# Rotary scores as 128-row products, rotary queries ahead of the heads, and a written order on four engines where attention hands over to decode and w_o

## The chip, the cores and the metric

The kernel runs on one core of one Trainium2 chip. The metric is device time in microseconds of one execution. Engines are named as in the profile: PE (TensorE) multiplies matrices, DVE (VectorE) and ACT (ScalarE) work on tiles, POOL (GpSimd) and SP (SyncE) mostly issue DMAs here; each engine works through its own queue in order. PEclk is the clock that TensorE was granted, as a share of full speed.

## The reference, cut

One step of a two-layer decoder. Layer 0 is latent attention (MLA) over 1024 new prompt tokens and, for 8 sequences with 4 new tokens each, over a paged cache of 8192 rows. Layer 1 is a gated DeltaNet, and each layer is followed by a SwiGLU FFN. Norms stand ahead of and behind every sublayer. What the change touches is layer 0:

```python
a = u @ w_in                                   # 1024 -> 384 + 256 + 64
c_q  = rmsnorm(a[..., :384], g_q)
c_kv = rmsnorm(a[..., 384:640], g_kv)
k_r  = rope(a[..., 640:], pos)                 # one rotary key of 64, shared by 8 heads
q = (c_q @ w_uq).reshape(b, t, 8, 128 + 64)    # per head: 128 plain + 64 rotary
q_rope = rope(q[..., 128:], pos)
s = (q_lat . c_kv + q_rope . k_r) * SCALE      # causal softmax over keys
...
o = (p @ c_kv) @ w_uv ;  mix = o @ w_o
h = x + rmsnorm(mix, nw1);  u = rmsnorm(h, nw2);  FFN(u)
```

## The kernel before

All products are in fp32 precision: each operand is split into a high part (ACT rounds it, `wh`, `qh`) and a low part (DVE subtracts, `wl`, `ql`), and three products hi·hi, lo·hi, hi·lo stand for one (L258, L259, L260 in `mm3`, called by `lin`). The split is `split` (L233 on ACT, L234 on DVE). Tokens are columns: groups GRP of 384, 384 and 288 (1024 prompt and 32 decode tokens). On PE the instructions stand in written order inside `order()`; the other engines' order, and that of PE outside, is set by the scheduler from the program.

**Projections** (`mla_latents`, until about 184 us). Behind the latents come four pairs of heads. For each pair: the pair's rotary queries (`mla_w_uqr`, three groups, ACT copies them to `qr`), then its two heads' plain queries (`mla_w_uqn`, each split into `qh`, `ql` and stored to DRAM `qd`). The rotation needs the swapped halves of `qr`: `swap` loads them by four DMAs (L602, issued on ACT's queue) into `araw`, and `rotate` makes three DVE passes (L607 to L609). `qrs` keeps the decode columns; high and low part go to DRAM `qrd`. The key's rotation (`raw[5]`) stands behind pair 1 and gives KRh (high part, in both halves of the rows) and KR (64 rows of high part, 64 of low part). Eight PSUM banks hold the projections.

**Prompt attention** (184 to 438 us, `mla_attend`). For each pair, `att_pair` loads its queries from DRAM on SP; `att_scores` scores 128 queries of one head against up to 512 keys a chunk: three plain products, one rotary product of the high query part on KR (128 rows: the query's high part stacked twice, so that both key parts count), the causal mask where the chunk holds the diagonal, and one rotary product of the low query part on KRh with 64 rows:

```python
mm(o, x["q1"][e][:, qsl], KR[:, c], start=False, stop=False)      # L1026
mm(o, x["q2"][r, qsl], KRh[r, c], start=False, stop=True)         # L1029, r: 64 rows
```

Then DVE takes the maximum, ACT the exponential, DVE normalises, PE transposes and multiplies with the values. Head outputs go to DRAM `oT`.

**Handover** (438 to 465 us). The heads come back from DRAM as `uo` (`oh`, `ol`), and `Decode` attends over the cache pages in 66 steps: `scores` (PE products L1746 to L1755, DVE maximum, ACT exponential `dpr`), `turn` (PE transposes L1790, ACT copies to `dpt`), `values` (PE, L1807). Two steps run first; then `wo_half` multiplies the first 768 columns by w_o, one column block `m` at a time, and `ffn_half` follows. In these, `aside` puts decode steps between the groups of products: each call does `turn`, adds RATE to a credit and does `scores` when it reaches one. POOL's order is written here, that of ACT, DVE and SP is the scheduler's.

**Norms** (`boundary_group`). Behind w_o come the sum of squares of the post-norm (on PE, L409), the residual (`hld` loads `xT` on SP, NHL buffers), squares `sqr` and, GAP groups later, the sum of the second norm, then `u`.

Of the kernel before, what the change touches and what calls it, by code (L numbers as in the profile page):

```python
# [15 lines left out]
P = 128  # L16
# [21 lines left out]
NHL = 5, 3  # L38
GAP = 1, 3
# [10 lines left out]
FW = (2, 3), (3, 4), (2, 4)  # L50
# [7 lines left out]
RATE = 0.55  # L58
# [45 lines left out]
class K:  # L104


    def __init__(self, ctx, tc, I, O):
# [8 lines left out]
        self.side, self.credit = None, 0.0  # L116
# [31 lines left out]
    def aside(self, middle=False):  # L148

        if self.side is None:  # L150
            return
        if middle:
            self.side.values()
            return
        self.side.turn()
        self.credit += RATE
        if self.credit >= 1 and self.side.scores():
            self.credit -= 1
# [103 lines left out]
    def lin(self, out, w, x, col, g, m=P):  # L262
# [7 lines left out]
        self.aside()  # L270

# [365 lines left out]
    def first_layer(self, right, top, h1, h2):  # L637
# [4 lines left out]
        with ExitStack() as left:  # L642
# [19 lines left out]
            for h, d in [(7, 1), (5, 0), (5, 1)] + [(h, d) for h in (0, 1, 2, 3, 4, 6, 7) for d in range(2)]:  # L662
                uo[h][d].half(0)
            acc, hid = ([Two(lambda: self.half(self.aa, 0, F32, "acc", 8), lambda i=i: self.half(self.ab[i], 1, F32, "acc", 8))
                         for _ in range(KD)] for i in range(2))
            with self.banks(**DBANK):
                with self.order(mybir.EngineType.Pool):


                    self.side = Decode(self, *smp, OL, tab, msk, wk)  # L670
                    pages = self.side.load

                    def heads(eng, *hd):
                        for h, d in hd:
                            eng.dma_start(uo[h][d].half(0).bitcast(F32), oT[h][d][:, :TA])

                    heads(nc.sync, (6, 0), (6, 1), (7, 0))
                    pages(1, 1, 0, 2, False)
# [3 lines left out]
                    pages(0, 1, 0, 4)  # L682
                    pages(1, 1, 2, 3)
                    heads(nc.gpsimd, (0, 0), (0, 1), (1, 0), (1, 1), (2, 0), (2, 1), (3, 0), (3, 1), (4, 0))
                    pages(0, 0, 0, 3)
                    pages(1, 1, 3, 4)
                    pages(0, 0, 3, 4)
                    heads(nc.sync, (7, 1))
                    heads(nc.gpsimd, (4, 1), (5, 0), (5, 1))
                    pages(1, 0, 0, 4)  # L690
                    for _ in range(2):
                        self.side.scores()
                        self.side.turn()
                        self.side.values()
                with self.order():
                    u, r2, start = self.boundary(acc, I["xT"], h1, (0, 1), (0, 2), uo, full)
                    self.kstep = KSTEP[1]
                    self.wo_half(uo, acc, gA, start, first)
# [8 lines left out]
                    for _ in range(9):  # L707
# [6 lines left out]
        with self.scope("ab") as self.ab[0], self.weights(*FW[1], side="left"), self.order(), self.banks(ps=8), \  # L714
                self.scope("ffn", "right") as self.fp:
            self.queue, self.gap = nc.gpsimd, GAP[1]
            for h, x in enumerate(uo):
                for d in range(2):
                    nc.sync.dma_start(x[d].half(1)[:, :TP - TA].bitcast(F32), oT[h][d][:, TA:])
# [14 lines left out]
    def wo_half(self, uo, acc, gs, start, first=()):  # L734
# [3 lines left out]
        first = list(first)  # L738
        for g in gs:
            for m in range(KD):  # L740
                ps = self.psum()
                self.lin(ps, self.weight(self.I["mla_w_o"][m], raw=first.pop(0) if first else None), uo, 0, g)
# [47 lines left out]
    def mla_latents(self, u, r2, start, ws, araw, gn, wk, cst):  # L790
        nc, I, O, tc, NH = self.nc, self.I, self.O, self.tc, 8
        with self.banks(ps=8):
# [32 lines left out]

            ckv = [(self.S(F32R, "kvh"), self.S(F32R, "kvl")) for _ in range(2)]
            KRh, KR = self.S(F32R, "KRh"), self.S(F32R, "KR")
# [8 lines left out]
            for p in range(NH // 2):  # L836
                qr, sw = self.S(F32, "qr"), araw(p % 2)
                for h in (None, 2 * p, 2 * p + 1):
                    w = self.weight(I["mla_w_uqr"][p] if h is None else I["mla_w_uqn"][h], 384)
                    if h is not None:  # L840
                        hl = self.S(F32R, "qh"), self.S(F32R, "ql")
                    for g in GRP:
                        self.ready(("q", g[0]))
                        ps = self.psum()
                        self.lin(ps, w, cq, 0, g)
                        n = min(g[1], TP - g[0])
                        s = slice(g[0], g[0] + n)
                        if h is None:
# [1097 lines left out]
```

## Time and profile before

| | |
|---|---|
| median of 3 runs | 3182.97 us (3180.69 to 3184.98) |
| profiled execution | 3181.79 us, its span 3180.1 us |
| granted clock, mean over the span | 0.978 |
| PE busy | 3062.9 us, 96% |
| DVE, ACT, POOL busy | 1835.7, 1170.1, 493.8 us |
| DMA | 432.42 MB, mean 136 GB/s |

In rows of the timeline the first number is the start in us, the second the duration (which overlaps the next for pipelined matmuls), then engine, line, operation, out<-in, shapes, and in brackets the idle time ahead of it with what ended it. A row of a window has its length, then busy us and instructions of PE, PE's weight loads, DVE, ACT and POOL, then PEclk, the DMA engines' share and GB/s.

### The profile page before, as it was taken

What the parts mean: (1) busy time and instruction counts of PE and PEld (TensorE: products, weight loads), DVE (VectorE), ACT (ScalarE), POOL (GpSimd) and SP (SyncE); (2) the same over time, 40 slices, a digit from 0 to 9 for tenths busy, and PEclk for the clock granted to TensorE, in tenths of its full rate; (3) what the DMA queues carried; (4) which work ended last, traced back from release to release, by engine and by line L of the source; (5) the groups of instructions that cost most, each with busy time, mean ns of one, the idle gap of its engine ahead of it and who ended that gap; (6) DMA issues with size and microseconds to landing.
All of it is one profiled execution on the core that took longest, in us unless ns stands there. A gap on an engine that the chain in (4) does not pass through costs nothing.

```text
span 3180.1 us, 57805 instructions
## 1 busy us (share of the span) xinstructions
PE 3062.9 (96%) x21526; PEld 2807.7 (88%) x21526; DVE 1835.7 (58%) x4234; ACT 1170.1 (37%) x2545; POOL 493.8 (16%) x897
## 2 busy tenths in 40 slices
PE   8999979999999999999999999999989999999998
PEld 8878857788888889999898888888789999999997
DVE  7667745634444444786676666666476444444436
ACT  5344434553333323454344444443443111111122
POOL 1200123343334321121011111111000000000000
PEclk9989989999999999999999999999999999999999
DMA  3553369988788854365422222223341111111113
GB/s 123 195 186 98 110 198 308 294 276 268 243 263 273 265 184 144 105 226 174 129 63 81 71 73 63 65 76 104 96 139 60 54 40 54 40 54 40 40 54 110
DMA packets 284987, 432.42 MB, mean 136 GB/s; under 512 B 60513, under 2 KB 220129, under 8 KB 284706
## 3 DMA queue, kind: packets, MB, share of 16 engines
q1 hardware_dynamic: 219138, 272.41, 26.7%
q0 software_dynamic: 45232, 141.92, 13.8%
q10 hardware_dynamic: 20336, 14.39, 1.5%
q8 instruction: 170, 2.79, 0.4%
q14 instruction: 111, 0.91, 0.1%
HBM read 367.59 MB, written 58.30 MB: 134 GB/s over the span
## 4 chain that ended last, share of the span: by engine, by line
PE 83%; DVE 8%; DMA 4%; issue 2%; ACT 2%; SPq 1%; POOL 0%; DVEq 0%; ACTq 0%; POOLq 0%
PE ps L258 21%; PE ps L260 21%; PE ps L259 21%; PE po L1807 2%; PE sc L1751 2%; PE tp L1056 1%; DMA w<-ffn_w_in 1%; PE sc L1029 1%; DVE wl L234 1%; PE sc L1755 1%; PE sc L1023 1%; PE s L1626 1%; ACT ga L1410 1%; PE s L1623 1%; DMA w<-mla_w_o 1%
## 5 line engine op out<-in xcount | busy, mean ns | idle before, releaser
L258 PE MATMUL ps<-oh,wh 128*128 128x384 f32 (+1 forms) x2496 | 823.2, 330 | 2.5 <-ACT wh L233 1.5
L260 PE MATMUL ps<-oh,wl 128*128 128x384 f32 (+1 forms) x2496 | 810.5, 325 | 2.0 <-DVE wl L234 2.0
L259 PE MATMUL ps<-ol,wh 128*128 128x384 f32 (+1 forms) x2496 | 808.7, 324 | 0.0
L233 ACT ACTIVATE wh<-w 128x1024 fp32r<-128x1024 f32 (+3 forms) x302 | 300.2, 1002 | 647.9 <-PE ps L259 497.0
L258 PEld LDWEIGHTS ps<-oh,wh 128*128 128x128 f32 x2496 | 473.6, 190 | 31.6 <-issue 28.0
L260 PEld LDWEIGHTS ps<-oh,wl 128*128 128x128 f32 x2496 | 472.9, 189 | 2.8 <-DVE wl L234 2.7
L259 PEld LDWEIGHTS ps<-ol,wh 128*128 128x128 f32 x2496 | 473.1, 190 | 1.3 <-issue 0.8
L234 DVE TENSOR_TENSOR wl<-w,wh 128x1024 fp32r<-128x1024 f32 (+3 forms) x299 | 343.0, 1155 | 149.9 <-ACT wh L233 145.7
L1723 POOL DMA_DIRECT2D pg<-cache x524 | 286.8, 547 | 438.7 <-PE po L1807 345.4
L258 PE MATMUL ps<-uh,wh 128*128 128x384 f32 (+1 forms) x912 | 312.1, 343 | 7.6 <-ACT wh L233 7.6
L259 PE MATMUL ps<-ul,wh 128*128 128x384 f32 (+1 forms) x912 | 307.9, 338 | 1.6 <-DVE ul L340 1.6
L260 PE MATMUL ps<-uh,wl 128*128 128x384 f32 (+1 forms) x912 | 303.0, 332 | 1.5 <-POOL wl L234 1.5
L258 PE MATMUL ps<-hh,wh 128*128 128x384 f32 (+1 forms) x880 | 294.1, 336 | 0.2 <-ACT hh L233 0.2
L259 PE MATMUL ps<-hl,wh 128*128 128x384 f32 (+1 forms) x880 | 289.9, 330 | 0.2 <-DVE hl L234 0.2
L260 PE MATMUL ps<-hh,wl 128*128 128x384 f32 (+1 forms) x880 | 289.3, 329 | 0.0
L258 PEld LDWEIGHTS ps<-uh,wh 128*128 128x128 f32 x912 | 175.0, 192 | 11.4 <-ACT wh L233 7.6
L259 PEld LDWEIGHTS ps<-ul,wh 128*128 128x128 f32 x912 | 175.1, 192 | 4.4 <-DVE ul L340 2.6
L260 PEld LDWEIGHTS ps<-uh,wl 128*128 128x128 f32 x912 | 174.5, 191 | 3.7 <-POOL wl L234 2.0
L258 PEld LDWEIGHTS ps<-hh,wh 128*128 128x128 f32 x880 | 165.3, 188 | 11.6 <-issue 7.3
L259 PEld LDWEIGHTS ps<-hl,wh 128*128 128x128 f32 x880 | 166.0, 189 | 1.3 <-DVE hl L234 0.4
L260 PEld LDWEIGHTS ps<-hh,wl 128*128 128x128 f32 x880 | 165.8, 188 | 0.1
L555 DVE TENSOR_TENSOR acc<-acc,ps 128x384 f32<-128x384 f32 (+1 forms) x240 | 121.2, 518 | 66.4 <-PE ps L260 65.8
(432 smaller groups left out, 4939.8 us busy)
## 6 DMA issues: line engine op xcount, KB each, us to landing
pg<-cache SPq DMA_DIRECT2D x500, 160.0 KB, 3.7
pg<-cache POOLq DMA_DIRECT2D x512, 128.0 KB, 3.6
w<-ffn_w_in SPq DMA_DIRECT2D x86, 512.0 KB, 4.1
w<-ffn_w_in POOLq DMA_DIRECT2D x52, 512.0 KB, 3.8
w<-ffn_w_out SPq DMA_DIRECT2D x40, 512.0 KB, 4.9
w<-dn_w_in SPq DMA_DIRECT2D x32, 512.0 KB, 3.2
w<-ffn_w_out POOLq DMA_DIRECT2D x26, 512.0 KB, 3.6
qn<-qd SPq DMA_DIRECT2D x64, 128.0 KB, 2.4
```

Source lines behind the costliest of these rows:

```text
L233: self.nc.scalar.activation(hi, src, AF.Copy)
L234: (lo_eng or self.nc.vector).tensor_tensor(lo, src, hi.bitcast(F32), op=ALU.subtract)
L258: mm(out, ah, bh, start=(i == 0), stop=False)
L259: mm(out, ah, bl, start=False, stop=False)
L260: mm(out, al, bh, start=False, stop=(i == n - 1))
L555: nc.vector.tensor_tensor(acc[m][:, s], acc[m][:, s], po[:, :tn], op=ALU.add)
L1023: mm(o, qh, kh[:, c], start=True, stop=False)
L1029: mm(o, x["q2"][r, qsl], KRh[r, c], start=False, stop=True)
L1056: self.nc.tensor.transpose(ps[:, j * P:(j + 1) * P], prob[:, kb * P:(kb + 1) * P], self.ident)
L1723: (self.nc.sync, self.nc.gpsimd)[pool].dma_start(self.pages[step, part][c0 + i // 2][:, i % 2], I["cache"][bass.ds(page, 1)].rearrange("o ...
L1751: mm(row(ps, c)[:, :256].rearrange("p (g k) -> p g k", g=2), q(i, c), pgs[c][:, :, i * P:(i + 1) * P], start=i == 0, stop=False)
L1807: nc.tensor.matmul(row(po, c)[:, :256], pT[:, j * P + c * TS_:j * P + (c + 1) * TS_], v, start=j == 0, stop=t < 0 or j == 1)
```

## The change

1. Scores: the low query part, too, is loaded stacked twice and multiplied with KR as a 128-row product, behind the mask. KRh is no longer kept.
2. Projections: all four pairs' rotary queries come first, then the eight heads. `swap` is issued on POOL's queue. The rotation of a pair stands behind the next pair's products (that of pair 3 behind head 0), the key's behind head 1. Absorbed-key weights and the first key and value up-projection weights are fetched and split at head 5.
3. `oT` is two DRAM tiles for each head, so that the first 768 columns can be loaded once stored.
4. Handover: the order is written on POOL, ACT, DVE and SP as well (EARLY). Two decode scores come first (the second into a `ps` bank), three w_o weights are fetched ahead, and two column blocks of w_o take the heads one by one in the order COME (`lin_part`).
5. Numbers: RATE 0.45 in w_o and the first FFN step, then 0.56 (0.55 before); GAP of the first stage 2 (1); NHL 4 (5); FW[0] (3, 3) ((2, 3)).

```diff
-NHL = 5, 3
-GAP = 1, 3
+EARLY = tuple(getattr(mybir.EngineType, n) for n in ("Pool", "Activation", "DVE", "SP"))
+COME = 0, 1, 2, 3, 4, 6, 5, 7
+COMING = 3, 6
+NHL = 4, 3
+GAP = 2, 3
-RATE = 0.55
+RATE = 0.45, 0.56
...
-                with self.order(mybir.EngineType.Pool):
+                with self.order(*EARLY):
...
-                    first = [self.raw_weight(I["mla_w_o"][m]) for m in range(2)]
+                    first = [self.raw_weight(I["mla_w_o"][m]) for m in range(3)]
...
-                    for _ in range(2):
-                        self.side.scores()
-                        self.side.turn()
-                        self.side.values()
+                    side.scores()
+                    side.scores("ps")
+                    first[0] = self.weight(None, raw=first[0])
+                    side.turn()
+                    side.values()
+                    first[1] = self.weight(None, raw=first[1])
+                    side.turn()
+                    first[2] = self.weight(None, raw=first[2])
+                    side.values()
+
+                    g = GRP[0]
+                    pss = [self.psum() for _ in range(2)]
+                    for i, h in enumerate(COME):
+                        if i == COMING[0]:
+                            side.scores()
+                        if i == COMING[1]:
+                            side.turn()
+                        for ps, x in zip(pss, first):
+                            self.lin_part(ps, x, uo, h, g, i == 0, i == 7)
+                    side.values()
...
-            for p in range(NH // 2):
-                qr, sw = self.S(F32, "qr"), araw(p % 2)
-                for h in (None, 2 * p, 2 * p + 1):
...
-                        self.swap(sw, qr, nc.scalar)
...
-                self.rotate(qr, sw, cos, sin)
...
+            for p in range(NH // 2):
+                qr[p], sw[p] = self.S(F32, "qr"), araw(p % 2)
+                w = self.weight(I["mla_w_uqr"][p], 384)
...
+                self.swap(sw[p], qr[p], nc.gpsimd)
+                if p:
+                    turned(p - 1)
+            for h in range(NH):
+                w = self.weight(I["mla_w_uqn"][h], 384)
...
+                if h == 0:
+                    turned(3)
+                if h == 1:
+                    keys()
+                if h == 5:
+                    absorbed.extend(self.raw_weight(I["mla_w_ukT"][hh]) for hh in range(2))
...
-            mm(o, x["q1"][e][:, qsl], KR[:, c], start=False, stop=False)
             if c0 + cn == nk:
                 mm(ps[:, cn - P:cn], identr, maskr, start=False, stop=False)
-            mm(o, x["q2"][r, qsl], KRh[r, c], start=False, stop=True)
+            for d in range(2):
+                mm(o, x["qr"][e][d][:, qsl], KR[:, c], start=False, stop=d == 1)
```

`turned(p)` is the rotation, split and store of pair p; `keys()` swaps, rotates and splits `raw[5]` into KR. In the changed kernel the line numbers are higher: L233, L234 become L236, L237, L607 to L609 become L620 to L622, L1770/L1774 and L1793 become L1842/L1846 and L1865, L874 becomes L896.

PE in the prompt attention, one chunk with the mask; the rows before (`KR`, `KRh` keys, `Q` rotary queries, `qn` plain queries, `kh`, `kl` keys):

```order
1001 L1023 MATMUL sc_2292<-kh_1791,qn_1831 128x384
1002 L1024 MATMUL sc_2292<-kl_1792,qn_1831 128x384
1003 L1025 MATMUL sc_2292<-kh_1791,qn_1833 128x384
1004 L1026 MATMUL sc_2292<-KR_986,Q_1815 128x384
1005 L1028 MATMUL sc_2292<-maskr,identr 128x128
1006 L1029 MATMUL sc_2292<-KRh_985,Q_1821 128x384
```

The same engine and chunk now:

```order
1001 L1094 MATMUL sc_2303<-kh_1809,qn_1838 128x384
1002 L1095 MATMUL sc_2303<-kl_1810,qn_1838 128x384
1003 L1096 MATMUL sc_2303<-kh_1809,qn_1840 128x384
1004 L1098 MATMUL sc_2303<-maskr,identr 128x128
1005 L1100 MATMUL sc_2303<-KR_985,Q_1821 128x384
1006 L1100 MATMUL sc_2303<-KR_985,Q_1824 128x384
```

The 64-row product on KRh became a second 128-row product on KR, and the mask moved ahead of both.

ACT at the handover, before (`ot` output of the prompt attention, `dpr` exponentials of decode scores, `dal` rescale factor, `dpt` transposed exponentials, `wh` high part of a w_o weight):

```order
434 L233 ACTIVATE ot_5001<-po_4976 128x256
435 L1770 ACTIVATE dpr_5212,dst_5210<-dsc_5213,dst_5210 128x32
436 L1793 ACTIVATE dpt_5220<-pt_5218 32x128
437 L233 ACTIVATE wh_5331<-w_5090 128x1024
438 L233 ACTIVATE wh_5364<-w_5092 128x1024
439 L233 ACTIVATE wh_5455<-w_5453 128x1024
440 L1774 ACTIVATE dpr_5277,dst_5274<-sc_5228,dst_5274 128x256
441 L1775 ACTIVATE dal_5276<-dst_5210,dst_5274 128x1
442 L1793 ACTIVATE dpt_5286<-pt_5283 128x256
```

The same place now:

```order
429 L236 ACTIVATE ot_5023<-po_4998 128x256
430 L1842 ACTIVATE dpr_5238,dst_5236<-dsc_5239,dst_5236 128x32
431 L1846 ACTIVATE dpr_5293,dst_5290<-ps_5244,dst_5290 128x256
432 L1847 ACTIVATE dal_5292<-dst_5236,dst_5290 128x1
433 L236 ACTIVATE wh_5299<-w_5104 128x1024
434 L1865 ACTIVATE dpt_5305<-pt_5303 32x128
435 L236 ACTIVATE wh_5313<-w_5106 128x1024
436 L1865 ACTIVATE dpt_5320<-pt_5317 128x256
437 L236 ACTIVATE wh_5322<-w_5108 128x1024
```

Both exponentials now stand ahead of the weights, and the three weights between the copies of the transposes.

DVE in the projections, before (`qr` rotary queries of pair 1, `araw` swapped halves, `araw_595` the rotary key, `ql` low parts of queries, `wl` of weights, `KR` the low key part):

```order
238 L607 TENSOR_TENSOR qr_1218<-qr_1218,cos_170 128x1056
239 L608 TENSOR_TENSOR araw_1219<-araw_1219,sin_171 128x1056
240 L607 TENSOR_TENSOR araw_595<-araw_595,cos_170 128x1056
241 L609 TENSOR_TENSOR qr_1218<-qr_1218,araw_1219 128x1056
242 L608 TENSOR_TENSOR araw_1402<-araw_1402,sin_171 128x1056
243 L234 TENSOR_TENSOR ql_1397<-qr_1218,qh_1396 128x1024
244 L609 TENSOR_TENSOR araw_595<-araw_595,araw_1402 128x1056
245 L234 TENSOR_TENSOR wl_1508<-w_1505,wh_1507 128x384
246 L234 TENSOR_TENSOR wl_1570<-w_1567,wh_1569 128x384
247 L234 TENSOR_TENSOR wl_1613<-w_1610,wh_1612 128x384
248 L874 TENSOR_TENSOR KR_986<-araw_595,KRh_985 64x1056
```

The same engine now, behind head 0 (`qr_1226` is pair 3, `ql_1383` head 1, `ql_1442` head 2):

```order
237 L620 TENSOR_TENSOR qr_1226<-qr_1226,cos_170 128x1056
238 L621 TENSOR_TENSOR araw_1227<-araw_1227,sin_171 128x1056
239 L622 TENSOR_TENSOR qr_1226<-qr_1226,araw_1227 128x1056
240 L237 TENSOR_TENSOR ql_1371<-qr_1226,qh_1370 128x1024
241 L237 TENSOR_TENSOR ql_1383<-ps_1384,qh_1382 128x384
242 L237 TENSOR_TENSOR ql_1383<-ps_1396,qh_1382 128x384
243 L237 TENSOR_TENSOR ql_1383<-ps_1408,qh_1382 128x256
244 L620 TENSOR_TENSOR araw_595<-araw_595,cos_170 128x1056
245 L621 TENSOR_TENSOR araw_1423<-araw_1423,sin_171 128x1056
246 L622 TENSOR_TENSOR araw_595<-araw_595,araw_1423 128x1056
247 L896 TENSOR_TENSOR KR_985<-araw_595,KRh_1431 64x1056
248 L237 TENSOR_TENSOR ql_1442<-ps_1443,qh_1441 128x384
```

The rotations of pair 3 and of the key now stand behind heads 0 and 1, each ahead of the next head's low parts.

More of the change, by code (lines that the diff above doesn't have):

```diff
@@ L115, in __init__ @@
         self.job_bank = "ps"
-        self.side, self.credit = None, 0.0
+        self.side, self.credit, self.late = None, 0.0, False
         self.n = 0
@@ L155, in aside @@
         self.side.turn()
-        self.credit += RATE
+        self.credit += RATE[self.late]
         if self.credit >= 1 and self.side.scores():
@@ L270, in lin, with lin_part @@
         self.aside()
+    def lin_part(self, out, w, x, k, g, first, last):
+        t0, tn = g
+        wh, wl = (t[:, k * P:(k + 1) * P] for t in w)
+        xh, xl = (t[:, t0:t0 + tn] for t in x[k])
+        mm = self.nc.tensor.matmul
+        mm(out[:, :tn], wh, xh, start=first, stop=False)
+        mm(out[:, :tn], wh, xl, start=False, stop=False)
+        mm(out[:, :tn], wl, xh, start=False, stop=last)
     def rsqrt(self, y, x, n, eng=None):
@@ L706, in first_layer @@
                     steps = self.ffn_half(0, u, r2, hid, gA, end, 16, full)
-                    for _ in range(9):
+                    next(steps)
+                    self.late = True
+                    for _ in range(8):
                         next(steps)
@@ L732, in order, with wo_half @@
         return self.tc.manual_schedule(engines={mybir.EngineType.PE, *engines})
-    def wo_half(self, uo, acc, gs, start, first=()):
+    def wo_half(self, uo, acc, gs, start, done=(), first=None):
         self.slack = SLACK[0]
-        first = list(first)
         for g in gs:
             for m in range(KD):
-                ps = self.psum()
-                self.lin(ps, self.weight(self.I["mla_w_o"][m], raw=first.pop(0) if first else None), uo, 0, g)
+                if g is gs[0] and m < len(done):
+                    ps = done[m]
+                else:
+                    w, first = first or self.weight(self.I["mla_w_o"][m]), None
+                    ps = self.psum()
+                    self.lin(ps, w, uo, 0, g)
                 self.nc.scalar.activation(acc[m][:, g[0]:g[0] + g[1]], ps[:, :g[1]], AF.Copy)
@@ new lines, in mla_latents, with absorb @@
+            pss, absorbed = [], []
+            def absorb(hh):
+                if not pss:
+                    pss.extend(self.psum() for _ in range(2))
+                w = absorbed[hh]
+                for h4 in range(4):
+                    hs = slice((hh * 4 + h4) * TS_, (hh * 4 + h4 + 1) * TS_)
+                    for rt in range(2):
+                        nc.tensor.matmul(pss[rt][:, hs], w[:, h4 * 256 + rt * P:h4 * 256 + (rt + 1) * P], qs[:, hs],
+                                         start=True, stop=True)
@@ L905, in mla_latents @@
                                      src.rearrange("p (h b s) -> p b h s", b=DB, s=DS), AF.Copy)
-            return (qd, qrd), (ckv, KR, KRh), (QS, new, cn)
+            return (qd, qrd, first), (ckv, KR), (QS, new, cn)
     def mla_attend(self, SC, q, kv, cst):
@@ L999, in att_pair @@
             self.split(vh[:, s], vl[:, s], ps)
+            if kb == 6:
+                rotary(1, 1)
             yield
@@ L1731, in fetch, with scores @@
             self.get(step, part, 0, 4, not part)
-    def scores(self):
-        if not self.steps or self.turning:
+    def scores(self, bank=None):
+        if not self.steps or self.turning and not bank:
             return False
```

172 lines of the change are left out of this document (90 added, 82 removed).

## The prediction

> **What bounds the kernel now.** The page's busy shares come first, then the chain that ended last.
>
> ```profile
> PE 3062.9 (96%) x21526; PEld 2807.7 (88%) x21526; DVE 1835.7 (58%) x4234; ACT 1170.1 (37%) x2545; POOL 493.8 (16%) x897
> PE 83%; DVE 8%; DMA 4%; issue 2%; ACT 2%; SPq 1%; POOL 0%; DVEq 0%; ACTq 0%; POOLq 0%
> ```
>
> TensorE is busy for 3063 of 3180 us and carries 83% of the chain. So time can come from two places: products that take longer than they need, and the 117 us in which TensorE waits. The rest of the program (the DeltaNet layer and the second FFN, some two thirds of the span) is not touched. I read four places: the scores of the prompt attention, the handover from attention to w_o, the norm behind w_o, and the query projections. The timeline of TensorE for one chunk of scores, and the line that the change rewrites:
>
> ```profile
> 305.99 0.40 PE L1025 MATMUL sc<-kh,qn 128*128 128x512 f32 x1
> 306.22 0.40 PE L1026 MATMUL sc<-KR,Q 128*128 128x512 f32 x1
> 306.55 0.49 PE L1029 MATMUL sc<-KRh,Q 64*128 64x512 f32 x1
> 306.97 0.50 PE L1023 MATMUL sc<-kh,qn 128*128 128x512 f32 x1
> 307.31 0.40 PE L1024 MATMUL sc<-kl,qn 128*128 128x512 f32 x1
> ...
> L1029 PE MATMUL sc<-KRh,Q x96: 323/440/502, 184.8 to 427.1; 64*128 64x384 f32 x40, 64*128 64x512 f32 x32, 64*128 64x256 f32 x16, 64*128 64x128 f32 x8
> ```
>
> Durations overlap, so I read distances between starts. One 128-row product of 512 columns passes in 0.23 us (305.99 to 306.22). The one ahead of L1029 takes 0.33, L1029 itself 0.42, and the product behind it 0.34, although L1029 uses half the rows. The array seems to empty at each side of a 64-row product. There are 96 of them. Two windows, the first in the attention, the second of a stage of 128-row products alone:
>
> ```profile
> 350.00:400.00 50.00, 49.57 (x313) 40.53 (x311) 36.81 (x105) 24.34 (x71) 8.18 (x15) 1.00 0.42 129
> ...
> 800.00:1000.00 200.00, 200.00 (x1760) 169.30 (x1759) 85.25 (x171) 69.79 (x130) 77.50 (x143) 1.00 0.81 257
> ```
>
> In the attention TensorE is busy 49.57 of 50 us at full clock, VectorE 36.81 and the DMA engines 0.42. What TensorE saves there counts, until VectorE has no slack.
>
> **Attention: −28 us (−18 to −33).** Every 64-row product becomes a 128-row one behind the mask product, on the same KR tile as its neighbour. In its own slot that saves 0.42 − 0.23 = 0.19; I take the 512-column excess for all sizes, since emptying costs per product and not per column: 96 × 0.19 = 18. Ahead of it 0.33 − 0.23 = 0.10 where no mask stands between (32 chunks); where it does (64) I take 0.07, because the mask product is shorter and I read no pair of it here: 3.2 + 4.5 = 7.7. Behind it 0.11 where another score follows at once; often a shorter values product follows, so half, 0.06 × 96 = 5.8. Together 31.5. VectorE's share goes from 36.8 of 50 to 36.8 of 43.5 (attention of 253 us, 184.8 to 438.27, shortened by an eighth), or 0.85; I give back 3 us for places where its chain of maxima and norms comes last. Lower bound: the own slots alone, 18. Upper: 0.10 and 0.11 at most chunks with no loss, 33. The second stacked rotary operand adds about 2 MB of loads on SP's queue to the attention's 253 us; the DMA share of 0.42 covers that. The fourth operand's load (issued at key block 6) stands in the first pair behind twelve loads of qn on SP; if it is late, the first scores of that head wait some microseconds, which I count under the projections' range. KRh as a temporary, mask and identity in another pool, and oT in two DRAM tiles cost no instruction on TensorE.
>
> [...]
>
> **Handover: −16 us (−6 to −20.8).** Rows of four engines' timelines (TensorE, ScalarE, VectorE, SP's queue), then two windows:
>
> ```profile
> 438.27 0.40 PE L1746 MATMUL sc<-new,QS 128*32 128x32 f32 x24
> 440.27 0.28 PE L1790 MATMUL pt<-ident,dpr 128*32 128x128 f32 x1 [1.61 <-ACT dpr L1770]
> 440.91 0.86 PE L1807 MATMUL po<-cn,dpt 32*32 32x256 f32 x8 [0.36 <-ACT dpt L1793]
> ...
> 443.41 1.08 PE L1755 MATMUL sc<-pg,QS 128*32 128x128 f32 x16
> 461.64 0.69 PE L1790 MATMUL pt<-ident,dpr 128*128 128x128 f32 x2 [17.15 <-ACT dpr L1774]
> 461.99 0.67 PE L258 MATMUL ps<-oh,wh 128*128 128x384 f32 x1
> ...
> 465.85 1.07 PE L1807 MATMUL po<-pg,dpt 128*32 128x256 f32 x16
> ...
> 458.04 1.06 ACT L233 ACTIVATE wh<-w 128x1024 fp32r<-128x1024 f32 x1 [15.28 <-DMA w<-mla_w_o]
> 461.02 0.47 ACT L1774 ACTIVATE dpr<-sc,dst 128x256 f32<-128x256 f32 x1 [1.93 <-DVE dst L1773]
> ...
> 459.12 1.23 DVE L234 TENSOR_TENSOR wl<-w,wh 128x1024 fp32r<-128x1024 f32 x1 [14.61 <-ACT wh L233]
> 460.27 0.42 DVE L1772 TENSOR_REDUCE dmx<-sc 128x1 f32<-128x256 f32 x1
> ...
> 445.70 1.15 SPq L240 DMA_DIRECT2D w<-mla_w_o  x2
> ...
> 440.00:465.00 25.00, 7.22 (x52) 4.99 (x53) 4.68 (x7) 4.57 (x10) 5.99 (x11) 0.59 0.84 288
> 458.00:465.00 7.00, 3.36 (x11) 3.36 (x12) 1.99 (x4) 2.19 (x5) 0.00 (x0) 0.50 0.54 186
> ```
>
> The second step's scores are done at 444.5, yet its transpose starts at 461.64. The waits view blames the exponential, but that is only the last link: the third weight's load is issued at 445.70 and lands at 458, and its split stands ahead of the maximum on VectorE and of the exponential on ScalarE. From the first decode product (438.27) to the first product of w_o (461.99) pass 23.7 us.
>
> Afterwards both score steps stand first and both exponentials stand ahead of every weight. From T, the first decode product: scores of both steps (0.40, then 2.7 as from the end of the values at 441.8 to 444.5) until T + 3.1; maximum and exponential 1.4 (460.27 to 461.64), with 0.3 for the small factor behind them, until T + 4.8; two weight splits on ScalarE ahead of the second step's copy, 2.1, until T + 6.9; transpose to values 0.64 (440.27 to 440.91), the values themselves 1.07: T + 8.7, where w_o begins. That saves 15.0. The values product of 465.85 is then done too (1.07), and the window 458 to 465 with its 3.36 busy us at a clock of 0.50 loses 1.7 that mostly disappear; the new short waits should lose about as much again. Sum 16. All three weights are loaded ahead of the rest, so the split finds them. Upper end: every wait there (17.15 + 1.61 + 0.36 for the next copy) and the 1.7. Lower end: the DMA engines are at 0.84 here and moved 288 GB/s, so TensorE may next wait for the heads' loads: if 10 of the 16 come back so, 6 remain. I take 16, because COME asks for the heads in the order in which their loads are queued. Written order binds POOL, ScalarE, VectorE and SP: whatever is late holds all behind it on that engine, and the heads that come last (6 and 7) are what will be late next.
>
> **Norm behind w_o: −4 us (−12 to +4).**
>
> ```profile
> 538.15 1.44 PE L409 MATMUL ps<-ones,sqr 128*128 128x1 f32 x6 [5.29 <-DVE sqr L392]
> ...
> 530.00:540.00 10.00, 4.71 (x33) 3.98 (x26) 7.19 (x16) 4.05 (x8) 5.69 (x11) 0.84 0.99 323
> 540.00:550.00 10.00, 10.00 (x83) 8.34 (x83) 4.62 (x15) 2.73 (x5) 5.47 (x10) 0.82 1.02 373
> ...
> hld<-xT SPq DMA_DIRECT2D x16, 192.0 KB, 8.5
> ```
>
> The sums of the second norm wait 5.29 us for VectorE's squares. GAP 1 to 2 puts one more group of 24 products (4 us at the 4.46 that 27 such products take below) between them, and RATE 0.45 takes out one decode score step (2.8) against one more values product: 4 + 1.1 − 2.8 = 2.3 more cover, so the wait falls to 3.0. Less idle time should also spare most of the reduced clock (0.84 of 4.71 busy us and 0.82 of 10, 2.6 us lost): −1.7. Together −4. The bad end: one buffer less for hld, whose loads take 8.5 us, +4. The good end: the whole wait, both windows' clock, and some of two later waits. RATE moves decode steps later, but by my count of the written order the last one falls at call 117 of 122, before 116 of 124, so no step is left over; cost 0 while TensorE stays the bound.
>
> **Query projections: +3 us (−20 to +9).** TensorE, ScalarE's queue, VectorE, a window, and the landing times of the swap loads (L602):
>
> ```profile
> 115.51 0.60 PE L427 MATMUL ps<-ident,ny 128*128 128x128 f32 x3 [2.90 <-DVE ny L282]
> ...
> 146.01 0.44 PE L258 MATMUL ps<-cqh,wh 128*128 128x384 f32 x1 [0.56 <-DVE ql L234]
> ...
> 150.47 0.34 PE L258 MATMUL ps<-cqh,wh 128*128 128x384 f32 x1
> ...
> 157.01 0.40 PE L258 MATMUL ps<-cqh,wh 128*128 128x288 f32 x1 [3.21 <-ACT qr L849]
> ...
> 170.53 0.80 PE L258 MATMUL sc<-kvh,wh 128*128 128x512 f32 x1 [4.59 <-ACT wh L233]
> ...
> 139.78 5.05 ACTq L602 DMA_DIRECT2D araw<-qr  x4
> ...
> 151.77 1.26 DVE L607 TENSOR_TENSOR qr<-qr,cos 128x1056 f32<-128x1056 f32 x1 [4.23 <-DMA araw<-qr]
> 156.61 1.22 DVE L234 TENSOR_TENSOR ql<-qr,qh 128x1024 fp32r<-128x1024 f32 x1 [1.12 <-ACT qh L233]
> ...
> 157.00:175.00 18.00, 13.21 (x52) 11.64 (x53) 9.97 (x14) 7.51 (x19) 4.94 (x12) 0.53 0.98 308
> ...
> DMA to landing us min/median/max: 2.5/5.3/8.8
> ```
>
> The rows show 11.3 us of waits; with the half clock of 157 to 175 (0.53 over 13.2 busy us, 6.2 lost, and some before) about 20 could be won here at best. The order moves them rather than removes them. One head takes TensorE 4.46 us (146.01 to 150.47) and fills three of eight banks. A rotation takes VectorE 3 × 1.25 = 3.7, then it waits for ScalarE's high part (1.06, the duration of the same shape at 458.04) and makes the low part (1.22): 6.0, with a head's own low parts (1.3) 7.3 against 4.46. By the written order VectorE does four rotations, the latent norms and the weights' low parts ahead of head 0's low part, so banks run out at head 2 (wait 2.3), again behind the fourth rotation (2.6). Then `keys` stands ahead of head 2's low part. Its swap goes on POOL's queue behind four stores, issued about 141, landing 5.3 later, then 3.7 + 1.06 + 1.25: VectorE resumes at about 152.4, while TensorE has filled its banks at about 143: 10 us. With 2.1 at 115 and 1.3 at head 6, whose weights now share a queue with preloaded ones, 18 of waits and 4 to 5 of half clock stand against 20: +3. What improves: ScalarE no longer issues the swaps (5.05), and the first key weights are split early (4.59 gone). Ends: all waits gone, or `keys` delayed to the longest landing (8.8) and the fourth rotary load late too, +9.
>
> **Sum.** −28 − 16 − 4 + 3 = −45, against the profiled execution of 3181.8 (span 3180.1): 3136.8. That execution lies 1.2 below the median of 3183, so I say 3137.
>
> **Rivals.** *Projections clear too:* swaps landing in 2.5 us and early split keys remove the old waits (−13 for +3): 3121, chance 0.15. For it speaks ScalarE's freed queue, against it the four stores ahead of the swap. *VectorE sets the pace in attention:* its share of 0.85 hides short bursts, and half of 28 is lost: 3151, chance 0.15. *Heads' loads limit the handover* (−6): 3147, chance 0.05. *64-row products were the cheap ones:* if packing were at work, each replacement would cost half a slot, 96 × 0.115 = +11 in place of −28: 3176, at the edge of no change; the 0.42 against 0.23 denies it, 0.02. [...] *Slower:* denser 128-row products make the clock drop in the attention. Of 225 us left there, a clock below 0.83 gives back all 46, and 0.80 adds 56: 3193. Against it stand 1.00 in 350 to 400 and 1.00 over 200 us of 128-row products; 0.02. My forecast has 0.61.
>
> **Range.** Ends of single terms above it: 10 (attention), 10 (handover), 8, 6; taken as independent 17, and with the rival of VectorE and one more term at its end 25: 3162. Below: 5, 5, 8 and 23, together 25: 3112. The forecast's own range is 3122 to 3152. A measurement here tells 0.2% (6.4 us) from no change; faster holds all but the last two rivals: 0.96, 0.02 same, 0.02 slower.
>
> **What would show it.** Attention: starts of score products 0.23 apart throughout, and the stage 25 to 31 us shorter. Handover: some 9 us from first decode product to first of w_o. Projections: VectorE waiting for the swap of raw[5] near 146, with TensorE idle about 10 us. I am wrong if VectorE's maxima or the rotary loads show up as releasers of TensorE in the attention, if w_o waits for oh or ol, or if the granted clock there drops below 1.00.

## The result, and the profile after

The changed kernel took 3148.2 us (median of 4 runs, 3136.75 to 3155.4) against 3181.83 us before (3177.58 to 3184.98): a ratio of 0.9892, interval 0.9857 to 0.9927. A repeat on another chip gave 3146.59 against 3185.12, ratio 0.989 (0.987 to 0.9911). So the change saves 34 to 39 us, where 45 were forecast; the time lies in the stated range. The profiled run shown here is the fastest of its four (3136.75, span 3135.1), which by itself would look like exactly 45. Why that is chance is shown below.

The page's busy shares and the chain that ended last, after:

```profile
PE 3022.0 (96%) x21526; PEld 2800.6 (89%) x21526; DVE 1830.4 (58%) x4234; ACT 1174.2 (37%) x2545; POOL 495.3 (16%) x909
PE 84%; DVE 8%; issue 3%; DMA 3%; ACT 2%; SPq 0%; POOL 0%; ACTq 0%; DVEq 0%; POOLq 0%
```

TensorE issues as many instructions as before and is busy 41 us less, while its idle time falls only from 117 to 113 us: old waits went, new ones came. From the starts of marked products in TensorE's timeline (first score, first decode product, first w_o product, and the 3001st product with a weight counted from there, products of the decode left out; it lies in the first half of the FFN, in the first step behind the end of the decode, which uses the tiles `oh` and `ol` again for its input):

| stage, us | before | after | repeat | gain | forecast |
|---|---|---|---|---|---|
| until the first score | 184.2 | 192.8 | 191.4 | −8.6, −7.2 | −3 |
| prompt attention | 254.0 | 229.2 | 230.7 | 24.8, 23.3 | 28 |
| handover to w_o | 23.7 | 7.2 | 8.7 | 16.5, 15.0 | 16 |
| w_o, norms, first FFN half up to the mark, decode | 749.2 | 745.6 | 744.8 | 3.6, 4.4 | 4 |
| rest of the program | 1969 | 1960 | 1963 | 9, 6 | 0 |

The four stages that the change touches give 36.4 and 35.7 us. TensorE's timeline of a chunk of scores, after (the two rotary products share one row, x2):

```profile
294.23 0.39 PE L1095 MATMUL sc<-kl,qn 128*128 128x512 f32 x1
294.46 0.40 PE L1096 MATMUL sc<-kh,qn 128*128 128x512 f32 x1
294.69 0.62 PE L1100 MATMUL sc<-KR,Q 128*128 128x512 f32 x2
295.15 0.39 PE L1094 MATMUL sc<-kh,qn 128*128 128x512 f32 x1
295.38 0.40 PE L1095 MATMUL sc<-kl,qn 128*128 128x512 f32 x1
```

Starts are 0.23 us apart throughout, and the two rotary products take 0.46 together (294.69 to 295.15) where 0.33 + 0.42 stood before. TensorE's waits in the projections and at the start of the attention, with the VectorE, POOL and SP rows behind them:

```profile
134.12 0.61 PE L261 MATMUL ps<-cqh,wh 128*128 128x288 f32 x1 [4.42 <-DVE ql L237]
157.44 0.61 PE L261 MATMUL ps<-cqh,wh 128*128 128x288 f32 x1 [11.34 <-DVE ql L237]
199.42 0.44 PE L1100 MATMUL sc<-KR,Q 128*128 128x128 f32 x1 [4.60 <-DMA Q<-qrd]
...
150.48 1.26 DVE L620 TENSOR_TENSOR araw<-araw,cos 128x1056 f32<-128x1056 f32 x1 [8.26 <-DMA rowsT<-araw]
...
142.52 0.53 POOL L934 DMA_DIRECT2D qd<-ql  x1 [0.21 <-issue]
143.05 1.48 POOL L615 DMA_DIRECT2D araw<-araw  x3
...
185.93 8.40 SPq L1025 DMA_DIRECT2D qn<-qd  x12
194.57 1.09 SPq L1025 DMA_DIRECT2D Q<-qrd  x2
```

Three of the four transfers of the key's swap are issued at 143.05, behind the stores of `qrd` and `qd` (the first had gone out at 139.47), and VectorE rotates at 150.48 (the view names a store of the latent rows as what ended its wait; the swap's last transfer was issued just ahead of that), and TensorE waits 11.34 us. At 199 the fourth rotary operand is late: its two loads go out at 194.57, behind twelve loads of qn. The handover, in rows of TensorE and ScalarE:

```profile
421.96 0.40 PE L1818 MATMUL sc<-new,QS 128*32 128x32 f32 x24
426.67 0.63 PE L1879 MATMUL po<-cn,dpt 32*32 32x256 f32 x8 [2.42 <-ACT dpt L1865]
428.16 1.07 PE L1879 MATMUL po<-pg,dpt 128*32 128x256 f32 x16 [0.48 <-ACT dpt L1865]
429.16 0.55 PE L281 MATMUL ps<-oh,wh 128*128 128x384 f32 x1
...
424.77 0.47 ACT L1846 ACTIVATE dpr<-ps,dst 128x256 f32<-128x256 f32 x1 [0.86 <-DVE dst L1845]
425.43 1.04 ACT L236 ACTIVATE wh<-w 128x1024 fp32r<-128x1024 f32 x1
```

One wait of 2.42 us and one of 0.48 stand where 17.15 stood. The norm behind w_o, then windows: the projections up to the wait of 11.34 us, and what follows it (three windows); the attention at its late operand, and further on; and behind the handover:

```profile
507.36 0.83 PE L422 MATMUL ps<-ones,sqr 128*128 128x1 f32 x6 [0.66 <-DVE sqr L405]
...
120.00:146.00 26.00, 20.51 (x109) 19.35 (x107) 15.68 (x18) 8.45 (x18) 12.82 (x32) 0.87 0.72 250
157.00:163.00 6.00, 5.55 (x20) 5.56 (x21) 3.79 (x9) 3.29 (x13) 3.23 (x6) 0.50 0.69 272
157.00:175.00 18.00, 16.73 (x86) 16.63 (x87) 8.35 (x18) 7.76 (x22) 4.28 (x8) 0.74 0.66 256
195.00:205.00 10.00, 4.83 (x18) 3.94 (x19) 3.56 (x13) 3.19 (x11) 0.00 (x0) 0.66 0.86 232
350.00:400.00 50.00, 48.46 (x347) 45.29 (x346) 41.04 (x124) 28.19 (x82) 9.99 (x18) 1.00 0.47 153
440.00:465.00 25.00, 25.00 (x173) 22.64 (x173) 9.71 (x15) 10.55 (x19) 4.38 (x8) 1.00 0.87 297
```

The wait of 5.29 for the second norm's sums is 0.66. From 350 to 400 VectorE is busy for 41.04 of 50 us and TensorE still for 48.46, at full clock. Behind the idle 11.34 us the clock is 0.50 until 163: half rate for the 6 us from 157 on, with TensorE busy for 5.55 of them.

### The profile page after: what moved, and what is told of

It reads as the page before. It is cut to its first block, busy times and chain, and to the rows that moved or that the text cites. A ratio compares the mean times of both kernels' runs of the same rounds, so it can differ in the third digit from the quotient of the medians.

```text
span 3135.1 us, 57855 instructions
## 1 busy us (share of the span) xinstructions
PE 3022.0 (96%) x21526; PEld 2800.6 (89%) x21526; DVE 1830.4 (58%) x4234; ACT 1174.2 (37%) x2545; POOL 495.3 (16%) x909
## 4 chain that ended last, share of the span: by engine, by line
PE 84%; DVE 8%; issue 3%; DMA 3%; ACT 2%; SPq 0%; POOL 0%; ACTq 0%; DVEq 0%; POOLq 0%
PE ps L261 22%; PE ps L262 21%; PE ps L263 21%; PE po L1879 2%; PE sc L1823 2%; PE sc L1100 1%; PE sc L1827 1%; PE tp L1127 1%; PE s L1698 1%; ACT ga L1482 1%; PE s L1695 1%; DVE wl L237 1%; PE ps L422 1%; PE s L1686 1%; PE ga L1605 1%
## 5 line engine op out<-in xcount | busy, mean ns | idle before, releaser
L236 ACT ACTIVATE wh<-w 128x1024 fp32r<-128x1024 f32 (+3 forms) x300 | 299.2, 1004 | 618.5 <-PE ps L262 523.0
L237 DVE TENSOR_TENSOR wl<-w,wh 128x1024 fp32r<-128x1024 f32 (+3 forms) x297 | 342.1, 1159 | 126.8 <-ACT wh L236 124.6
```

Of the source, the lines that this page charges most:

```text
L236: self.nc.scalar.activation(hi, src, AF.Copy)
L237: (lo_eng or self.nc.vector).tensor_tensor(lo, src, hi.bitcast(F32), op=ALU.subtract)
```

## The experiments

Theory: the attention gains what the 64-row products cost; the projections and the fourth rotary load give part of it back; the rest of the program only scatters. Rivals stand with each run. "Gain" below is that of the profiled run over the profiled run before, at the 3001st product with a weight, so that the scatter behind it is left out; the changed kernel has 36.4 and 35.7 there.

**The changed kernel again.** No edit.

> The changed kernel unaltered, against the kernel before. Its profiled run was 45 us faster than the profiled run before, the median of its four runs only 34. Theory A: the work itself gains about 35 us, and the profiled run won another 8 to 15 us in the DeltaNet layer (1540 to 2290 us), which is not changed, because less of its time fell under a lowered clock. Then this profile shows the projections at +8, attention at -25, handover at -16 and w_o to the end of the first FFN at -4 as before, and differs in the DeltaNet layer; median 3140 to 3150. Theory B: 45 is the real gain and the other runs were disturbed elsewhere; then the median falls to 3137 and the DeltaNet layer is again some 8 us shorter than before.

Measured: 3146.59 (3140.34 to 3164.93), and the stages in the table. The changed stages repeat within 2 us. The rest of the program was 6 us shorter than before this time (9 in the first profile), but in other kernels here, which leave it as the changed kernel has it, it was up to 10 us longer. Two parts of it scatter. The DeltaNet layer, up to its first output product, took 662 us before, 654 and 656 in these two profiles, and 655 to 665 in the other kernels with the changed code; what follows it took 960 to 972. What stands ahead of it, layer 0's second half, took 345 to 347 in all of them. A place where this happens: in the DeltaNet layer TensorE waits for a load of YT in some profiles and not in others. From the kernel called "both2" below, its wait and the window behind it, then the same window of time in the changed kernel, which has no such wait there:

```profile
2194.06 1.22 PE L1606 MATMUL ga<-YT,U 128*128 128x128 f32 x4 [5.03 <-DMA YT<-yt]
...
2197.00:2217.00 20.00, 18.15 (x156) 15.39 (x156) 4.88 (x14) 8.78 (x27) 0.00 (x0) 0.67 0.23 72
```

```profile
2197.00:2217.00 20.00, 15.85 (x171) 12.72 (x171) 6.48 (x20) 9.99 (x32) 1.44 (x1) 1.00 0.10 30
```

Wait and lowered clock together make some 8 us of difference: "both2" is 1.9 us later ahead of the wait (a product of `smp` starts at 2179.33 against 2177.43) and 9.5 us behind it (the last product of the layer's recurrence at 2226.50 against 2216.99). Theory A holds for the stages and the median. Its other half, that the DeltaNet layer's gain is chance, this run alone does not show, since the layer was shorter again; the kernels below, in which it was longer with the same code, do. What decides whether that load is late was not settled.

**The first part alone, on the kernel before** ("rot"; here its edit in the scores).

```diff
-            mm(o, x["q1"][e][:, qsl], KR[:, c], start=False, stop=False)
             if c0 + cn == nk:
                 mm(ps[:, cn - P:cn], identr, maskr, start=False, stop=False)
-            mm(o, x["q2"][r, qsl], KRh[r, c], start=False, stop=True)
+            for d in range(2):
+                mm(o, x["qr"][e][d][:, qsl], KR[:, c], start=False, stop=d == 1)
```

> The kernel before with the first part of the change alone: two 128-row rotary products behind the mask, four stacked operands, the fourth loaded at key block 6, mask and identity in the attention's own buffers. Theory A (emptying of TensorE at each 64-row product): the prompt attention from its first score to the first decode product is 25 to 31 us shorter than 254, plus a wait of up to 5 us for the fourth operand; the whole 20 to 30 us faster than before. Rival B (VectorE sets the pace): 10 to 15. Rival C (a 64-row product costs half a 128-row one): no faster.

Measured: 3164.78 (3162.1 to 3165.86), ratio 0.9932 (0.9919 to 0.9945), 20 us faster. The attention went from 254.0 to 225.7 us, a gain of 28.4; the fourth operand was waited for only 0.80 us here. Rivals B and C fall. The gain at the 3001st product is 19.7: some 8 us were lost again, among them 1 us at the handover, whose old wait was 19.64 us in this kernel instead of 17.15, 2.8 in two waits for a decode exponential, and 3.2 where the FFN waits for its first weight behind the decode (4.70, 1.48 before). Why an edit in the attention lengthens these waits is not shown.

**Each 64-row product twice** ("twice", on the kernel before; the low part then counts twice).

```diff
+            mm(o, x["q2"][r, qsl], KRh[r, c], start=False, stop=False)
             mm(o, x["q2"][r, qsl], KRh[r, c], start=False, stop=True)
```

> The kernel before with each 64-row rotary product issued twice in a row (the low part then counts twice in the scores). Theory A (TensorE empties when the row count changes): the second of the two follows at the pace of any product, about 0.23 us at 512 columns, and the two slots of 0.33 and 0.34 around stay. Theory B (a 64-row product is slow in itself): the second takes 0.42 again. Rival C (it costs half a 128-row one): 0.12.

TensorE's timeline of this kernel, one chunk without mask:

```profile
315.77 0.40 PE L1025 MATMUL sc<-kh,qn 128*128 128x512 f32 x1
316.00 0.40 PE L1026 MATMUL sc<-KR,Q 128*128 128x512 f32 x1
316.33 0.50 PE L1029 MATMUL sc<-KRh,Q 64*128 64x512 f32 x1
316.67 0.39 PE L1030 MATMUL sc<-KRh,Q 64*128 64x512 f32 x1
316.99 0.50 PE L1023 MATMUL sc<-kh,qn 128*128 128x512 f32 x1
317.33 0.40 PE L1024 MATMUL sc<-kl,qn 128*128 128x512 f32 x1
317.56 0.40 PE L1025 MATMUL sc<-kh,qn 128*128 128x512 f32 x1
```

The slots from 316.00 are 0.33, 0.34, 0.32, 0.34 and then 0.23. One 64-row product had 0.42 between two changes; two have 0.34 + 0.32 = 0.66, so the second adds 0.24: a 64-row product costs here what a 128-row one does (0.23). Each change of the row count adds about 0.10 to the slot ahead of it and to the one behind it (0.33 and 0.34 against 0.23). The attention grew by 16.5 us for 96 products. Theory A holds, B and C fall: the price goes with the change of the row count. That the array empties there is the reading of it that the prediction gave; the slots show the time, not what fills it.

**The key's swap earlier, keys behind head 3** ("keys"), and the same with the fourth operand loaded early ("both").

```diff
+                if p == 1:
+                    ksw = araw(2)
+                    self.swap(ksw, raw[5], nc.gpsimd)
...
-                sw = araw(0)
-                self.swap(sw, raw[5], nc.gpsimd)
-                self.rotate(raw[5], sw, cos, sin)
+                self.rotate(raw[5], ksw, cos, sin)
...
-                if h == 1:
+                if h == 3:
                     keys()
```

> The changed kernel, but the key's swap is issued behind pair 1's into another buffer (that of the latent query), and its rotation stands behind head 3 in the program. Theory A (the swap's transfer behind four stores on POOL's queue makes VectorE, and so TensorE, wait 11.3 us at 157): that wait goes to 3 us or less, the wait at 134 grows from 4.4 to at most 8 because the scheduler now places the key's rotation ahead of head 0, and the half clock behind it shrinks: 6 to 12 us faster than the changed kernel. Rival B (VectorE and ScalarE simply have too much to do there, the swap is only the last link): the waits move and their sum stays at 16 us or more; 0 to 3 us faster.

> As the kernel with the early key swap, and the first pair's fourth rotary operand is loaded with the other three instead of at key block 6. Theory A: the wait of 4.6 us for it at 199 goes, with nothing in its place: 4 to 5 us faster than the early swap alone. Rival B: the loads on SP's queue are late as a whole (the queue issues without pause from 175 to 199), so the plain queries behind it are late instead; within 2 us of the early swap alone.

"keys" took 3155.71 (3148.45 to 3157.27), no faster than the changed kernel, where theory A asked for 6 to 12 us. Its projections did what theory A says: the wait of 11.34 is gone, the first score comes at 184.4, 7 to 8 us earlier, and the attention ends as much earlier. But the lead was lost behind it: TensorE waits 6.83 us for a page of the cache, and the gain at the 3001st product is 31.4. "both" took 3141.94 (3140.9 to 3146.11); its attention is 222.5 us against 230.0, and the page wait is there too (6.29). So the early fourth operand is worth 7.5 us. That is more than the wait itself, 5.24 in "keys", because the clock behind the wait falls too. The window around it, in "keys" and then in "both":

```profile
186.00:204.00 18.00, 12.76 (x60) 11.21 (x59) 8.71 (x32) 5.84 (x19) 0.00 (x0) 0.81 0.78 201
...
186.00:204.00 18.00, 17.58 (x110) 15.88 (x111) 14.01 (x46) 9.61 (x30) 0.00 (x0) 1.00 0.89 244
```

A clock of 0.81 over 12.76 busy us loses 2.4.

**The same two with keys left behind head 1** ("keys2", "both2"). The edit of "both2" beside that of "keys2":

```diff
-        for e, d in ((0, 0), (0, 1), (1, 0)):
+        for e, d in ((0, 0), (0, 1), (1, 0), (1, 1))[:4 - (p > 0)]:
             rotary(e, d)
...
-            if kb == 6:
+            if kb == 6 and p:
                 rotary(1, 1)
```

> The changed kernel with the early key swap only: the swap behind pair 1's, the rest of keys stays behind head 1, so that the tiles are handed out in the order of the changed kernel. In the kernel that moved keys behind head 3 the cache pages' loads on POOL's queue began at 414 instead of 387 to 403, and TensorE waited 6.8 us for a page. Theory A (that came from tiles handed out in another order, not from the earlier start): here the pages' loads are issued before the attention ends, no page wait over 1.5 us, first score near 184.5 and all of the 7 to 8 us stay: 5 to 9 us faster than the changed kernel. Rival B (an earlier attention meets the same transfers): the page wait is here too, and the gain by the end of the first FFN is below 3 us.

> The early key swap with keys behind head 1, and the first pair's fourth rotary operand loaded with the other three. Theory A: 4 to 5 us faster than the early swap alone, attention 253 - 28 = 225 us long or a little less, about 46 to 48 us faster than before by the end of the first FFN; rival B: pages or heads are late instead, and at most 42.

"keys2" took 3148.71 (3137.76 to 3150.59), "both2" 3145.73 (3144.82 to 3150.72); first scores at 184.1 and 184.4, attention 229.3 and 221.9 us, gains 36.5 and 43.0. The page wait stayed (7.78 in "keys2"), so the place of `keys` was not its cause; my theory A for "keys2" fell in that point. For "both2" the attention is shorter than the 225 that theory A asked for, but the gain of 43.0 lies between the 46 of theory A and the 42 of rival B, and pages are late, as rival B had it. TensorE's wait in "both2" and the POOL row that issues the load, then the POOL rows of the repeat of the changed kernel for the same loads:

```profile
428.57 1.03 PE L1824 MATMUL sc<-pg,QS 128*32 128x256 f32 x2 [7.51 <-DMA pg<-cache]
...
406.58 3.49 POOL L1796 DMA_DIRECT2D pg<-cache  x6 [44.80 <-PE po L1146]
```

```profile
386.89 1.15 POOL L1795 DMA_DIRECT2D pg<-cache  x2 [1.57 <-issue]
403.53 2.30 POOL L1795 DMA_DIRECT2D pg<-cache  x4 [15.49 <-DMA oT<-ot]
```

With the early swap POOL stands 44.80 us in front of a page load until the attention's last product is done. In the built program the buffer of one of those pages overlaps the values of the last pair; in the changed kernel it overlaps a rotary operand that is read earlier. Moving the swap's instructions in the projections had handed the buffers out in another order.

**Both repairs, buffers shifted** ("both3").

```diff
+            for _ in range(13):
+                nc.gpsimd.memset(self.S(F32, "dm")[:, :1], 0.0)
             with self.order():
```

> As the kernel with both repairs, with 13 one-column writes to passing tiles ahead of the attention, which shift which buffer each later tile gets. In the two kernels with the early key swap the sixth page's load on POOL's queue waited for the last product of the attention (413.6), because its buffer was that of the last pair's values; here, as in the changed kernel, it is that of a rotary operand that is read earlier. Theory A (the page wait of 7.5 us comes from that buffer alone): the page loads are issued some 15 us or more before the attention ends, the page wait is below 2 us, the gain by the end of the first FFN goes from 43 to 47 to 52 us. Rival B (an earlier attention meets the same transfers anyway): page wait 5 us or more, gain at most 44.

Measured: 3132.13 (3125.16 to 3135.62), ratio 0.9825 (0.9803 to 0.9848). Its interval lies below that of the changed kernel on either chip, and it is the fastest kernel of this study. The longest page wait is 1.49 us, and POOL no longer waits for the attention's last product; TensorE's wait, then POOL's later page loads:

```profile
423.38 1.08 PE L1826 MATMUL sc<-pg,QS 128*32 128x256 f32 x8 [1.49 <-DMA pg<-cache]
...
388.05 1.14 POOL L1798 DMA_DIRECT2D pg<-cache  x2 [23.24 <-DMA oT<-ot]
392.84 3.80 POOL L1798 DMA_DIRECT2D pg<-cache  x6 [1.50 <-issue]
```

These loads go out at 388 to 397, 10 to 18 us ahead of the attention's end at 406.3, and the gain at the 3001st product is 50.1 instead of 43.0. Theory A holds: with other buffers, and no other change than the 13 short writes that shift them, the page wait of 7.51 us goes.

**The handover with POOL's order alone written** ("pool").

```diff
-EARLY = tuple(getattr(mybir.EngineType, n) for n in ("Pool", "Activation", "DVE", "SP"))
+EARLY = tuple(getattr(mybir.EngineType, n) for n in ("Pool",))
```

> The changed kernel with the written order at the handover on POOL alone; the scheduler then puts the three splits of w_o's weights ahead of the second exponential on ScalarE again. The weights are still fetched early. Theory A (the wait of 17 us before was the third weight's late load, with the order only passing it on): about three splits later, 2 to 4 us slower than the changed kernel. Rival B (the order itself is what counts): 10 us or more slower.

Measured: 3153.03 (3150.23 to 3159.51); the handover is 10.7 us instead of 7.2 and 8.7, with waits of 2.71 and 1.84, and the gain 32.5 instead of 36.4 and 35.7. ScalarE's rows show the three splits of the weights ahead of the second exponential again:

```profile
425.25 2.93 ACT L236 ACTIVATE wh<-w 128x1024 fp32r<-128x1024 f32 x3
...
430.44 0.47 ACT L1846 ACTIVATE dpr<-ps,dst 128x256 f32<-128x256 f32 x1 [2.10 <-DVE dst L1845]
```

Theory A holds: the written order on ScalarE, VectorE and SP is worth 2 to 3.5 us of the handover and 3 to 4 at the 3001st product. The other 13 us of the handover's gain remain without it, with the weights fetched ahead and both scores first in the program; which of these two gives how much was not tried.

**GAP and RATE as before** ("nums").

```diff
-GAP = 2, 3
+GAP = 1, 3
-RATE = 0.45, 0.56
+RATE = 0.55, 0.55
```

> The changed kernel with GAP 1 and RATE 0.55 throughout, as before; NHL stays 4. Theory A (the longer gap and the slower rate cover the second norm's sums): TensorE waits 4 to 6 us there again, 2 to 6 us slower by the end of the first FFN. Rival B (the smaller rate only defers decode steps, which are paid for at the end of the decode): within 2 us.

Measured: 3159.88 (3151.16 to 3163.88); gain 26.4, so the two numbers together are worth 9 to 10 us, more than either theory said; GAP and RATE were not tried apart. The wait is back, longer than before, and the clock behind it is low:

```profile
512.59 1.44 PE L422 MATMUL ps<-ones,sqr 128*128 128x1 f32 x6 [7.99 <-DVE sqr L405]
...
510.00:520.00 10.00, 7.41 (x55) 6.06 (x56) 6.84 (x21) 2.21 (x6) 5.24 (x10) 0.62 0.92 290
```

## Why the prediction was right, and where it was off

The time lies in the range, and most steps went as described. But two of the four terms (attention and norm) came out near their forecast only because misses in them cancel, and one sign of being wrong that the prediction named did appear.

*Attention, −28.* The slots were right: 0.19 in the product's own slot and 0.10 at each side ("twice"). The emptying to which the sum puts them down no run shows; the runs show that the time goes with the change of the row count. Taking the 0.19 for all sizes was right too: in the profile before, the 64-row product's own slot is 0.31, 0.37 and 0.43 us at 256, 384 and 512 columns, where a 128-row one has 0.12, 0.18 and 0.23. The 3 us given back for VectorE were not needed: with all four operands in time ("both2") the attention is 221.9 us, a gain of 32, near the upper bound of 33. Against that stands the step that failed, the fourth rotary operand. The prediction saw that its load stands behind twelve loads of qn and still priced it at nothing in the sum; it cost 7.4 us ("keys2" against "both2"). It said that it would be wrong if the rotary loads showed up as releasers of TensorE in the attention, or if the clock there dropped: both happen at 199 (4.60 us for Q, then 0.66 from 195 to 205). So the net 23 to 25 is a sum of two errors of opposite sign, and that it lies near 28 is partly luck.

*Handover, −16.* Measured 16.5 and 15.0; the forecast path of 8.7 us took 7.2 and 8.7 (the clock from 426 to 431 was 0.83 in the first profile, 0.60 in the repeat). The heads' loads did not limit it. Behind it, among the first w_o products, the page loads did cost time as soon as the attention ended earlier (7.51 us in "both2"), which no rival of the prediction had named.

*Norm behind w_o, −4.* Measured 3.6 and 4.4 for the whole stage, which is luck. The numbers alone are worth 10 us ("nums"); with them as before, the same stage took 756.3 us, 7 more than in the kernel before. Of these 7, 4 lie in one wait of the FFN, for its first weight behind the decode. The kernel before, TensorE and POOL of the changed kernel:

```profile
1186.85 0.54 POOL L240 DMA_DIRECT2D w<-ffn_w_in  x1 [26.82 <-DVE hl L234]
...
1167.47 0.69 PE L261 MATMUL ps<-oh,wh 128*128 128x384 f32 x1 [5.59 <-ACT wh L236]
...
1161.21 0.54 POOL L243 DMA_DIRECT2D w<-ffn_w_in  x1 [28.83 <-PE pt L1902]
```

Before, that weight was loaded 15 us ahead of the decode's last transposes, and TensorE waited 1.48 us; now the load goes out only behind them, and the wait is 5.59. RATE is not the reason: the wait is 5.49 in "nums", which has the old RATE, and 4.70 in "rot". What moved the load is open.

A price in the prediction's sum was wrong as well: a decode score step stands there with 2.8 us, which is what the second step shows (up to 444.5). The clock was 0.50 there; at full clock the same 32 products take 1.44 (473.12 to 474.56):

```profile
441.20:444.60 3.40, 3.29 (x40) 1.38 (x32) 2.69 (x3) 1.55 (x2) 1.62 (x3) 0.50 0.96 247
...
473.12 1.07 PE L1751 MATMUL sc<-pg,QS 128*32 128x256 f32 x16
474.01 0.62 PE L1755 MATMUL sc<-pg,QS 128*32 128x128 f32 x16
474.56 0.44 PE L258 MATMUL ps<-oh,wh 128*128 128x384 f32 x1
...
472.00:476.00 4.00, 4.00 (x47) 3.21 (x47) 1.86 (x3) 1.96 (x3) 0.01 (x1) 1.00 0.74 230
```

So taking one such step out costs half as much cover as the sum has it: by its own working the cover is 3.7 us instead of 2.3, and the wait falls to 1.6 instead of 3.0; measured is 0.66.

The lead on the way misleads, too. At the 661st product, ahead of the decode's end, it had grown by 14 us since the first w_o product. But 13 decode steps had been scored by then and 12 finished, instead of 15. At 1.44 us for scores and 1.0 for values these are an estimated 6 us that are paid later; with the 4 of the late weight about 4 remain. So the prediction's "cost 0" for RATE is not refuted; what it missed is the late weight and the size of what GAP and RATE save together.

*Projections, +3.* Measured +8.6 and +7.2. The mechanism was right to the place: the swap (three of its four transfers) behind four stores, VectorE resuming at 150.5 (forecast 152.4) and a wait of 11.34 (10). The two small waits missed in opposite directions (4.42 in place of 2.3, and under 0.8 in place of 2.6) and nearly cancel. The size was off in the clock: 0.87 over 20.5 busy us (120 to 146) and 0.74 over 16.7 (157 to 175) lose about 7 us, where 4 to 5 were allowed. The wait for the swap was 1.3 longer as well.

*Rivals.* The projections did not clear; VectorE did not set the pace (0.82 of the window 350 to 400, the largest wait for it in the attention 0.98 us); the clock was 1.00 in that window, so denser products did not lower it there. The rival of cheap 64-row products rests on a packing, and on half a slot (0.115 us) for each product, that no run shows; in "twice" the second of two 64-row products took 0.24 us, where a 128-row one takes 0.23. Summed, the missing 9 us of 45 are 4 to 6 in the projections and 3 to 5 in the attention.

## What to carry to other kernels

A product that used half the rows among full ones cost here a full product (0.24 us against 0.23) and about 0.10 us at each of two changes of the row count; a duplicated operand that makes it full was the cheaper form (attention 28.4 us shorter in "rot") as long as its load was on time (a late one cost 7.4 us). When a stage is made to end earlier, look next at what was preloaded beneath it, and at who used the buffers of these loads last: in "both2", behind an edit in the projections, POOL stood 44.80 us in front of a page load until the attention's last product was done, and with other buffers ("both3") the loads went out 10 to 18 us ahead of that end. And judge a change of one per cent at marked points in the program, not by one run's total, when an untouched part of it scatters by some 10 us either way. A mark can mislead as well, where work that is done in between (here decode steps) has only been put off.

## What the runs showed that was not expected

- A lone 64-row product of 512 columns among 128-row ones cost 0.40 us more than a 128-row one, which has 0.23: 0.10 in the slot ahead, 0.19 in its own, 0.11 in the one behind (kernel before, 306.22 to 307.31). The second of two in a row cost 0.24 ("twice").
- Moving one swap ahead in the projections turned page loads that were issued by 403 ("again") into ones that waited until 413.58 ("keys2"), and TensorE then stood idle for 7.8 us.
- The untouched rest of the program took between 1960 and 1980 us in the profiles of these kernels.
